# Fetching each expert's tokens by indirect DMA instead of one-hot products in a mixture-of-experts kernel, with the weight splits on fixed engines

## The chip, the cores and the metric

The kernel runs on one core of a Trainium2 chip, in one launch. Its time is the device time of a whole execution in microseconds (us). The core has TensorE (PE, matrix products, with a separate row PEld for its weight loads), VectorE (DVE), ScalarE (ACT), GpSimd (POOL) and SyncE (SP, which here only issues DMAs). DMAs issued by SP go through queue q1 of the profile, those issued by GpSimd through queue q0.

## The reference, cut to what matters

The whole model is two transformer-like blocks over 512 latent tokens and 256 context tokens of width 1024. The change lies in the mixture of experts at the end of the first block. Each token chooses one of 4 groups and 2 of the 4 experts in it; every expert is a gated MLP of width 512:

```
gates = sum(one_hot(expert_id, 16) * top_w)          # (512, 16), two entries a token
for e in range(16):
    a = silu(t @ w_gate[e]) * (t @ w_up[e])          # 1024 -> 512
    y = y + gates[:, e:e + 1] * (a @ w_down[e])      # 512 -> 1024
```

## The kernel before, in words

**Precision.** Every fp32 product is made of three fp32r products. An operand x is split into a high part (a rounded copy of x) and a low part (x minus the high part), and `mm3` (L526 to L530) multiplies high by high, high by low and low by high. So each weight that comes from DRAM is split on the chip before it is used: `unit` (L507) takes a loaded 1 MB unit of weights and cuts it into two pieces of 128x1024; for each piece `split` (L265) makes the high part `whi` (L268 on ScalarE, or L270 on another engine) and then the low part `wlo` (L271). `split_on` is a list of engine pairs that the pieces use in turn. In the expert stage it has four entries, so that of four pieces one has its high part made by VectorE and one has its low part made by GpSimd; ScalarE makes the other high parts and VectorE the other low parts.

**Buffers.** Loaded units lie in 6 buffers of 1 MB (`wraw`, `wrawx`), the split pieces in 4 buffers each of `whi` and `wlo`. SP issues the load of a unit when its buffer comes free; that is the order written in the program, so a load that waits holds those behind it. Three units of gate and up weights for the first experts are loaded ahead (`self.early`).

**The router stage** (`moe`, L1343 to L1372) makes the normalised tokens h (feature by feature), turns them token by token on TensorE and keeps them in SBUF as a high part `hthi` (`hhi`, 4 blocks of 128 tokens by 1024 features) and a low part `htlo`. It then computes the router's choices: `posm` is for each token and expert its place among that expert's tokens (or -1), and `tw` holds token numbers and weights. An expert takes up to 128 tokens at a time, in 128 slots; more than 128 tokens go through `moe_overflow`, a loop whose count is read on the chip (none in the profiled data; the engines meet at the branch).

**The expert stage** (L1442 to L1470) takes the 16 experts in pairs. For a pair, `gather(e)` builds one-hot matrices of tokens by slots (`slot_onehot`, L1237, VectorE). `gather_slots` (L1241) then multiplies `hthi` and `htlo` by them on TensorE: 8 feature blocks, 2 parts and 4 token blocks, so 64 products of 256 columns (128 slots of two experts), whose results ScalarE (six of eight) and VectorE (two of eight) copy to `sxg`. `slot_rows` (L1307) makes from the same one-hots, with 4 products and 2 small transposes, each slot's token number `sri` and weight `srw`. For each expert `hidden` (L1258) makes 48 products of 512 columns for gate and up (8 pieces of weights), `turned` (L1279) transposes the result, and `down` (L1290) makes 24 products (4 pieces), scales the two halves by the slot's weight on ScalarE and VectorE (L1302, L1303), and adds the 128 rows of 4 KB to `ysd` in DRAM by an indirect DMA from GpSimd's queue (L1304). The loop runs `hidden` of expert e+1 between `turned` and `down` of expert e. `late` (after expert 13) reloads the context's normalised tokens, 2 MB, into the memory of `hthi`.

**Order.** The order of the instructions on each engine's queue is fixed when the program is built, by a scheduler that models their times; engines work through their queues in that order.

Of the kernel before, what the change touches and what calls it, by code (L numbers as in the profile page):

```python
# [21 lines left out]
P = 128  # L22
# [201 lines left out]
class Kern:  # L224
# [1016 lines left out]
    def gather_slots(self, pool, oh, hh, name):  # L1241

        nc = self.nc
        n = oh.shape[2]
        x = []
        for k in range(KD):
            if k % 2 == 0:
                x.append(pool.tile([P, 2, 2, n, P], F32R, name=name + "xg", bufs=4))
            p = self.ps.tile([P, 2, n * P], F32, name="aux", tag="aux")
            for i in range(2):  # L1250
                for j in range(4):
# [6 lines left out]
    def hidden(self, pool, x, i, wg, wu, bufs=2):  # L1258

        nc = self.nc  # L1260
        pp = []
        for w in (wg, wu):
            p = self.mmp.tile([P, 512], F32, name="mm")
            for k0 in (0, 4):
                for kp, m, whi, wlo in self.unit(w, k0, 4, [(0, 512)]):
                    for k in range(m):
                        kk = k0 + kp + k
                        xk = x[kk // 2][:, kk % 2]
                        self.mm3(p, xk[:, 0, i, :], xk[:, 1, i, :], whi[:, k, :], wlo[:, k, :], kk == 0, kk == 7)
# [20 lines left out]
    def down(self, pool, a, wd, ysd, slot, bufs=2):  # L1290
# [12 lines left out]
        nc.vector.tensor_scalar(y[:, 512:], py[1], slot[1], None, op0=ALU.mult)  # L1303
# [3 lines left out]
    def slot_rows(self, pool, oh, tw, name):  # L1307
# [14 lines left out]
        for i in range(n):  # L1322
            v = p[:, i, 3 * i:3 * i + 3]
            w = pool.tile([P, 2], F32, name=name + "rw", bufs=4)
            nc.vector.tensor_scalar(w[:, 1:2], v[:, 0:1], 0.0, self.c["part"], op0=ALU.is_equal, op1=ALU.mult)
            row = pool.tile([P, 1], I32, name=name + "ri", bufs=4)
# [5 lines left out]
    def moe(self, dp, hhi, late, ysd, x, bs, mod, fill):  # L1332
# [8 lines left out]
        hh = [hhi, rp.tile([P, 4, D], F32R, name="htlo")]  # L1341
        with self.phase():
# [4 lines left out]
            for i, b in enumerate(bs):  # L1347
                j0, ts = 2 * i, slice(i * 256, i * 256 + 256)
                for k in range(KD):
# [10 lines left out]
                    if k % 2:  # L1360
                        at = lambda t: t[:, j0:j0 + 2, (k - 1) * P:(k + 1) * P]
                        self.split(at(hh[0]), at(hh[1]), p.rearrange("p j k e -> p j (k e)"))
# [78 lines left out]
        self.moe_overflow(dp, hh, ysd, tw, posm, ovl)  # L1441
        with self.phase():  # L1442
            ep = self.pool("exp", 1)
            self.split_on = [(None, None), (None, None), (None, nc.gpsimd), (nc.vector, None)]

            def gather(e):
                oh = self.slot_onehot(ep, posm[:, :, e:e + 2], "s")
                yield self.gather_slots(ep, oh, hh, "s")
                yield self.slot_rows(ep, oh, tw[:, :, e:e + 2, :], "s")
            w = self.weights  # L1450
            xg, rows = gather(0)
            *_, a = self.hidden(ep, xg, 0, w("w_gate", 0), w("w_up", 0))
            for e in range(16):
                slot, g, steps = rows[e % 2], None, None
                if e % 2 and e < 15:
                    g = gather(e + 1)
                    xg = next(g)
                if e < 15:
                    steps = self.hidden(ep, xg, (e + 1) % 2, w("w_gate", e + 1), w("w_up", e + 1))
                    if not g:  # L1460
                        next(steps)
                at = self.turned(ep, a)
                if g:
                    rows = next(g)
                if steps:
                    *_, a = steps
                self.down(ep, at, w("w_down", e), ysd, slot)
                if e == 13:
                    late()
            self.split_on = [(None, None)]  # L1470
# [21 lines left out]
    def moe_overflow(self, dp, hh, ysd, tw, posm, ovl):  # L1492
# [5 lines left out]
        with tc.If(nov > 0), self.phase():  # L1498
# [8 lines left out]
            with tc.For_i(0, nov) as i, self.phase():  # L1507
# [10 lines left out]
                x = self.gather_slots(lp, oh, hh, "o")  # L1518
                w = lambda n: self.weights(n, e)
                *_, a = self.hidden(lp, x, 0, w("w_gate"), w("w_up"), 1)  # L1520
# [361 lines left out]
def build(tc, aps):  # L1882
    nc = tc.nc
    with ExitStack() as ctx:
# [14 lines left out]
        ysd = sd.tile([T + P, D], F32, name="ysd")  # L1899
        mn = K.vec("mix_norm_2", 0, 8)  # L1900
        with K.phase():
# [80 lines left out]
            with K.phase(4):  # L1982
# [6 lines left out]
                for j in range(5):  # L1989
                    nc.sync.dma_start(ysd[j * P:j * P + P, :], z)  # L1990
                xc, accc = K.load_x(cp, aps["ctx_2"], TC, "xcT")
# [12 lines left out]
        with K.phase():  # L2004
            K.wlp = K.pool("wl", 4)
            with K.phase(5, 0, 4):
                K.moe(sd, hhi, reload_hc, ysd, x, bs, mod, lambda pool: ada0(K.matvec_steps, range(5, 6), pool, 2, True))
# [72 lines left out]
```

## Time and profile before

| | |
|---|---|
| median of 3 runs | 2445.67 us (2443.76 to 2450.09) |
| the profiled execution | 2448.05 us, of which the span from first to last instruction is 2446.0 us |
| busy over the span | PE 94%, DVE 69%, ACT 47%, POOL 30% |
| mean granted TensorE clock | 0.981 of full speed |
| expert stage | from about 777 us to the last indirect DMA's issue at 1158.5 us |

Busy shares of the whole span are averages over stages with different limits; what matters for the change is the expert stage, a sixth of the span. The pages give, for a stretch, how many us each engine was busy and the mean share of time that the 16 DMA engines were busy. The spans of products overlap, since they are pipelined: the pace of TensorE is read from the distance of their starts.

### The profile page before, as it was taken

What the parts mean: (1) busy time and instruction counts of PE and PEld (TensorE: products, weight loads), DVE (VectorE), ACT (ScalarE), POOL (GpSimd) and SP (SyncE); (2) the same over time, 40 slices, a digit from 0 to 9 for tenths busy, and PEclk for the clock granted to TensorE, in tenths of its full rate; (3) what the DMA queues carried; (4) which work ended last, traced back from release to release, by engine and by line L of the source; (5) the groups of instructions that cost most, each with busy time, mean ns of one, the idle gap of its engine ahead of it and who ended that gap; (6) DMA issues with size and microseconds to landing.
All of it is one profiled execution on the core that took longest, in us unless ns stands there. A gap on an engine that the chain in (4) does not pass through costs nothing.

```text
span 2446.0 us, 36705 instructions
## 1 busy us (share of the span) xinstructions
PE 2294.4 (94%) x14498; PEld 1975.1 (81%) x14498; DVE 1694.9 (69%) x2552; ACT 1159.8 (47%) x1910; POOL 737.0 (30%) x502
## 2 busy tenths in 40 slices
PE   6998989989987999998999999999999999999998
PEld 4988978768875777777997888877888998888887
DVE  4777877778855999998684884897483435653553
ACT  4454654456753555555435764432343333442443
POOL 2124544345331445444160333232333001010111
PEclk9999999999998999999999999999999999999999
DMA  8563003251054788898410003566343222223221
GB/s 310 180 222 136 27 27 124 79 208 42 2 186 168 269 307 292 294 306 296 150 62 13 1 1 121 196 216 218 137 147 112 91 101 72 87 82 116 91 84 58
DMA packets 65390, 344.40 MB, mean 141 GB/s; under 512 B 7728, under 2 KB 12480, under 8 KB 33984
## 3 DMA queue, kind: packets, MB, share of 16 engines
q1 hardware_dynamic: 62032, 331.32, 37.5%
q0 software_dynamic: 3184, 10.72, 2.7%
q8 instruction: 115, 1.88, 0.3%
q14 instruction: 59, 0.48, 0.1%
HBM read 326.06 MB, written 16.78 MB: 140 GB/s over the span
## 4 chain that ended last, share of the span: by engine, by line
PE 49%; DVE 12%; issue 4%; POOL 2%; ACT 1%; DMA 0%; SPq 0%; POOLq 0%; DVEq 0%; ACTq 0%
PE mm L529 14%; PE mm L530 14%; PE mm L528 13%; DVE wlo L271 4%; DVE mva L383 2%; PE aux L1252 2%; DVE whi L270 1%; PE sc L1578 1%; PE av L1721 1%; PE aux L1596 1%; PE av L1712 1%; POOL ysd L1304 1%; POOL wlo L271 1%; DVE smax L1585 1%; DVE cy L1835 0%
## 5 line engine op out<-in xcount | busy, mean ns | idle before, releaser
L528 PE MATMUL mm<-hhi,whi 128*128 128x512 f32 (+1 forms) x1184 | 438.9, 375 | 10.1 <-ACT whi L268 5.3
L529 PE MATMUL mm<-hlo,whi 128*128 128x512 f32 (+1 forms) x1184 | 442.3, 375 | 2.9 <-DVE hlo L480 2.9
L530 PE MATMUL mm<-hhi,wlo 128*128 128x512 f32 (+1 forms) x1184 | 439.8, 374 | 0.0
L271 DVE TENSOR_TENSOR wlo<-wraw,whi 128x1024 fp32r<-128x1024 f32 (+1 forms) x187 | 271.6, 1461 | 176.1 <-ACT whi L268 174.3
L268 ACT CAST whi<-wraw 128x1024 fp32r<-128x1024 f32 (+1 forms) x224 | 231.9, 1038 | 331.3 <-PE mm L529 229.9
L271 DVE TENSOR_TENSOR wlo<-wrawx,whi 128x1024 fp32r<-128x1024 f32 (+1 forms) x158 | 220.7, 1423 | 96.7 <-ACT whi L268 95.3
L268 ACT CAST whi<-wrawx 128x1024 fp32r<-128x1024 f32 (+1 forms) x178 | 185.4, 1043 | 213.3 <-PE mm L530 105.6
L530 PE MATMUL mm<-whi,hlo 128*128 128x256 f32 x960 | 275.0, 289 | 4.8 <-DVE hlo L480 4.6
L529 PE MATMUL mm<-wlo,hhi 128*128 128x256 f32 x960 | 275.2, 288 | 4.1 <-DVE wlo L271 4.1
L528 PE MATMUL mm<-whi,hhi 128*128 128x256 f32 x960 | 274.1, 287 | 5.3 <-ACT hhi L479 2.6
L528 PEld LDWEIGHTS mm<-hhi,whi 128*128 128x128 f32 x1184 | 225.6, 192 | 49.0 <-ACT whi L268 5.9
L529 PEld LDWEIGHTS mm<-hlo,whi 128*128 128x128 f32 x1184 | 226.9, 192 | 41.3 <-DVE hlo L480 3.3
L530 PEld LDWEIGHTS mm<-hhi,wlo 128*128 128x128 f32 x1184 | 226.2, 191 | 37.9 <-issue 0.2
L271 POOL TENSOR_TENSOR wlo<-wraw,whi 128x1024 fp32r<-128x1024 f32 (+1 forms) x53 | 148.4, 2799 | 262.7 <-ACT whi L268 218.9
L528 PEld LDWEIGHTS mm<-whi,hhi 128*128 128x128 f32 x960 | 186.5, 195 | 6.8 <-ACT whi L268 3.1
L530 PEld LDWEIGHTS mm<-whi,hlo 128*128 128x128 f32 x960 | 186.0, 195 | 7.3 <-DVE hlo L480 6.6
L529 PEld LDWEIGHTS mm<-wlo,hhi 128*128 128x128 f32 x960 | 186.7, 195 | 5.1 <-DVE wlo L271 5.0
L271 POOL TENSOR_TENSOR wlo<-wrawx,whi 128x1024 fp32r<-128x1024 f32 (+1 forms) x52 | 138.4, 2662 | 167.6 <-ACT whi L268 167.6
L1845 POOL TENSOR_TENSOR cy<-cy,csg 128x512 f32<-128x512 f32 x44 | 62.5, 1420 | 351.4 <-DVE cy L1837 342.4
L383 DVE SCALAR_TENSOR_TENSOR mva<-mvr,cc_c,mva 128x512 f32<-128x512 f32 x154 | 156.1, 1013 | 2.4 <-DMA mvr<-in_w_mod_dram 0.2
L529 PE MATMUL mm<-alo,whi 128*128 128x512 f32 (+1 forms) x396 | 145.1, 367 | 0.0
L528 PE MATMUL mm<-ahi,whi 128*128 128x512 f32 (+1 forms) x396 | 144.7, 366 | 0.0
(548 smaller groups left out, 4964.4 us busy)
## 6 DMA issues: line engine op xcount, KB each, us to landing
wrawx<-in_w_down_dram SPq DMA_DIRECT2D x32, 1024.0 KB, 5.2
wrawx<-in_w_gate_dram SPq DMA_DIRECT2D x30, 1024.0 KB, 5.0
wraw<-in_w_up_dram SPq DMA_DIRECT2D x30, 1024.0 KB, 5.0
wraw<-in_ffn_w_up_dram SPq DMA_DIRECT2D x30, 1024.0 KB, 4.9
mvr<-in_ada_w_dram SPq DMA_DIRECT2D x56, 512.0 KB, 4.5
wraw<-in_ada_w_dram SPq DMA_DIRECT2D x20, 1024.0 KB, 5.5
wraw<-in_w_in_dram SPq DMA_DIRECT2D x18, 1024.0 KB, 6.8
mvr<-in_w_mod_dram SPq DMA_DIRECT2D x32, 512.0 KB, 4.2
```

The source lines that it names most:

```text
L268: nc.scalar.copy(hi, src)
L270: hi_eng.tensor_copy(hi, src)
L271: (lo_eng or nc.vector).tensor_sub(lo, src, hi.bitcast(F32))
L383: nc.vector.scalar_tensor_tensor(acc, raw[:, k, :], c, acc, op0=ALU.mult, op1=ALU.add)
L528: nc.tensor.matmul(out, ahi, bhi, start=start, stop=False)
L529: nc.tensor.matmul(out, ahi, blo, start=False, stop=False)
L530: nc.tensor.matmul(out, alo, bhi, start=False, stop=stop)
L1252: nc.tensor.matmul(p[:, i, :], hh[i][:, j, k * P:k * P + P], oh[:, j].rearrange("p n s -> p (n s)"), start=j == 0, stop=j == 3)
L1304: nc.gpsimd.indirect_dma_start(out=ysd, out_offset=bass.IndirectOffsetOnAxis(ap=slot[0], axis=0), in_=y, in_offset=None, compute_op=ALU.add)
L1578: nc.tensor.matmul(s[:, a:a + n], qs[:, qt * P:qt * P + P], ks[i][:, a:a + n], start=i == 0, stop=i == 1)
L1585: nc.vector.tensor_reduce(m, s[:, :768], axis=AX.X, op=ALU.max, negate=True)
L1845: nc.gpsimd.tensor_mul(y, y, sg)
```

## The change

Tokens are no longer gathered by products. The router stage keeps no high and low parts of the turned tokens; it copies them once in fp32 (`ht`, on ScalarE) and stores them to a new DRAM tensor `hd` (four DMAs of 512 KB on SP's queue). Per pair of experts the one-hots and `slot_rows` stay, for the row numbers. With these, `gather_slots` issues one indirect DMA per expert on GpSimd's queue, which reads 128 rows of 4 KB from `hd` into `xt` (2 buffers); a slot without a token reads a row of zeros, stored once beforehand. `slots_feature` turns `xt` feature by feature with 8 transposes on TensorE and splits the result from PSUM into high parts (ScalarE) and low parts (VectorE), two operations of 128x512 each. The gathers are issued for the pair after the next expert, so about one expert ahead of their use. `split_on` is no longer set in this stage: all high parts of weights are made by ScalarE, all low parts by VectorE. Both halves of an expert's result are scaled on ScalarE. `late` moves from after expert 13 to after expert 1. The diff, cut to its core:

```diff
-    def gather_slots(self, pool, oh, hh, name):
...
-                    nc.tensor.matmul(p[:, i, :], hh[i][:, j, k * P:k * P + P], oh[:, j].rearrange("p n s -> p (n s)"),
-                                     start=j == 0, stop=j == 3)
-            dst = x[-1][:, k % 2].rearrange("p i n s -> p i (n s)")
-            (nc.vector.tensor_copy if k % 4 == 3 else nc.scalar.copy)(dst, p)
-        return x
+    def gather_slots(self, pool, hd, row, bufs=2):
+
+        xt = pool.tile([P, D], F32, name="xt", bufs=bufs)
+        self.nc.gpsimd.indirect_dma_start(out=xt, out_offset=None, in_=hd,
+                                          in_offset=bass.IndirectOffsetOnAxis(ap=row, axis=0))
+        return xt
+
+    def slots_feature(self, pool, xt, bufs=2):
+
+        nc = self.nc
+        hi, lo = (pool.tile([P, KD, P], F32R, name="xg" + n, bufs=bufs) for n in ("hi", "lo"))
+        for k0 in (0, 4):
+            p = self.ps.tile([P, 4, P], F32, name="aux", tag="aux")
+            for k in range(4):
+                nc.tensor.transpose(p[:, k, :], xt[:, (k0 + k) * P:(k0 + k + 1) * P], self.ident)
+            self.split(hi[:, k0:k0 + 4, :], lo[:, k0:k0 + 4, :], p)
+        return hi, lo
...
-        nc.vector.tensor_scalar(y[:, 512:], py[1], slot[1], None, op0=ALU.mult)
+        nc.scalar.mul(y[:, 512:], py[1], slot[1])
...
-        hh = [hhi, rp.tile([P, 4, D], F32R, name="htlo")]
+        ht = rp.tile([P, 4, D], F32, name="ht")
...
-                        self.split(at(hh[0]), at(hh[1]), p.rearrange("p j k e -> p j (k e)"))
+                        nc.scalar.copy(ht[:, j0:j0 + 2, (k - 1) * P:(k + 1) * P], p.rearrange("p j k e -> p j (k e)"))
+                for j in (j0, j0 + 1):
+                    nc.sync.dma_start(hd[j * P:j * P + P, :], ht[:, j, :])
...
-            self.split_on = [(None, None), (None, None), (None, nc.gpsimd), (nc.vector, None)]
+            rows, xts = [], []
 
             def gather(e):
...
+                oh = self.slot_onehot(ep, posm[:, :, e:e + 2], "s", 1)
+                two = self.slot_rows(ep, oh, tw[:, :, e:e + 2, :], "s")
+                rows.extend(two)
+                xts.extend(self.gather_slots(ep, hd, row) for row, _ in two)
             w = self.weights
-            xg, rows = gather(0)
-            *_, a = self.hidden(ep, xg, 0, w("w_gate", 0), w("w_up", 0))
+            gather(0)
+            xg = self.slots_feature(ep, xts[0])
+            steps = self.hidden(ep, xg, w("w_gate", 0), w("w_up", 0))
+            next(steps)
+            xg = self.slots_feature(ep, xts[1])
+            gather(2)
+            *_, a = steps
             for e in range(16):
...
                 if e < 15:
+                    steps = self.hidden(ep, xg, w("w_gate", e + 1), w("w_up", e + 1))
+                    next(steps)
                 at = self.turned(ep, a)
+                if e < 15:
+                    next(steps)
+                if e < 14:
+                    xg = self.slots_feature(ep, xts[e + 2])
+                if e % 2 and e < 12:
+                    gather(e + 3)
+                if e < 15:
                     *_, a = steps
+                self.down(ep, at, w("w_down", e), ysd, rows[e])
+                if e == 1:
                     late()
```

The loop of `moe_overflow` uses the same two functions; its body does not run on this data.

## Rows read from the trace of the kernel before

**Rows 1.** Windows: busy us and instructions of each engine, clock, DMA share, GB/s.

```profile
930.00:976.00 46.00, 43.59 (x224) 35.42 (x223) 44.47 (x41) 25.13 (x31) 22.45 (x9) 1.00 0.87 297
```

**Rows 2.** Groups of VectorE, 838 to 1022 us: busy us, mean ns, idle before.

```profile
L271 DVE TENSOR_TENSOR wlo<-wrawx,whi 128x1024 fp32r<-128x1024 f32 x48 | 72.8, 1556 | 0.4
L271 DVE TENSOR_TENSOR wlo<-wraw,whi 128x1024 fp32r<-128x1024 f32 x24 | 49.8, 2098 | 1.4 <-ACT whi L268 1.1
L270 DVE CAST whi<-wrawx 128x1024 fp32r<-128x1024 f32 x16 | 24.0, 1498 | 1.9 <-PE mm L530 1.9
L1303 DVE TENSOR_SCALAR ey<-mm,srw 128x512 f32<-128x512 f32 x8 | 6.0, 747 | 1.9 <-PE mm L530 1.9
L1255 DVE CAST sxg<-aux 128x512 fp32r<-128x512 f32 x8 | 5.5, 688 | 0.7 <-PE aux L1252 0.7
L270 DVE CAST whi<-wraw 128x1024 fp32r<-128x1024 f32 x8 | 5.5, 688 | 0.0
...
L271 DVE TENSOR_TENSOR ealo<-aux,eahi 128x512 fp32r<-128x512 f32 x8 | 5.4, 677 | 0.0
```

**Rows 3.** Groups of ScalarE, 838 to 1022 us.

```profile
L268 ACT CAST whi<-wrawx 128x1024 fp32r<-128x1024 f32 x49 | 51.5, 1051 | 40.5 <-PE mm L530 40.5
L268 ACT CAST whi<-wraw 128x1024 fp32r<-128x1024 f32 x24 | 25.2, 1049 | 26.9 <-PE mm L530 23.3 <-DVE soh L1237 3.6
L1255 ACT CAST sxg<-aux 128x512 fp32r<-128x512 f32 x24 | 13.5, 581 | 1.3 <-PE aux L1252 1.3
L1302 ACT ACTIVATE ey<-mm,srw 128x512 f32<-128x512 f32 x8 | 5.5, 688 | 9.3 <-PE mm L530 9.3
```

**Rows 4.** Waits of SP's queue, 760 to 1170 us: total us, times, longest.

```profile
SPq L504 <- POOL wlo L271: 170.2, 46, 7.0
SPq L504 <- DVE wlo L271: 170.1, 88, 10.3
```

**Rows 5.** Timeline of TensorE in the expert stage.

```profile
784.27 0.40 PE L528 MATMUL mm<-whi,sxg 128*128 128x512 f32 x1
...
905.12 0.39 PE L530 MATMUL mm<-whi,sxg 128*128 128x512 f32 x1
...
906.48 0.39 PE L530 MATMUL mm<-whi,sxg 128*128 128x512 f32 x1
...
919.87 0.60 PE L1284 MATMUL aux<-cst,ea 128*128 128x128 f32 x4
```

**Rows 6.** Timeline of VectorE and GpSimd: start us, us, operation, idle before.

```profile
851.67 2.46 DVE L271 TENSOR_TENSOR wlo<-wraw,whi 128x1024 fp32r<-128x1024 f32 x2
851.78 2.55 POOL L1304 DMA_INDIRECT ysd<-ey,sri  x1 [6.09 <-DVE whi L270]
...
920.57 4.23 DVE L271 TENSOR_TENSOR wlo<-wraw,whi 128x1024 fp32r<-128x1024 f32 x1
...
920.74 2.97 POOL L271 TENSOR_TENSOR wlo<-wrawx,whi 128x1024 fp32r<-128x1024 f32 x1
```

**Rows 7.** The line of the indirect DMA: duration ns min/median/max, first and last start.

```profile
L1304 POOL DMA_INDIRECT ysd<-ey,sri x16: 1552/1770/2562, 825.7 to 1158.5; - x16
...
DMA to landing us min/median/max: 6.0/6.9/11.1
```

**Rows 8.** DMA queues, 838 to 1022 us: packets, MB, share of 16 engines.

```profile
q1 hardware_dynamic: 6885, 50.11, 71.8%
q0 software_dynamic: 1152, 4.19, 14.3%
```

**Rows 9.** DMA queues, 10 to 40 us.

```profile
DMA packets 2569, 12.43 MB, mean 414 GB/s; under 512 B 293, under 2 KB 293, under 8 KB 1505
...
q1 hardware_dynamic: 2560, 12.42, 101.1%
```

**Rows 10.** Timelines of VectorE and SP around the stage's begin.

```profile
777.14 1.29 DVE L1237 TENSOR_TENSOR soh<-cst,posm 128x512 fp32r<-128x512 f32 x2 [3.54 <-PEq L1498]
...
782.54 3.72 SPq L504 DMA_DIRECT2D wraw<-in_w_up_dram  x2
```

More of the change, by code (lines that the diff above doesn't have):

```diff
@@ L1239, in slot_onehot, with hidden @@
         return oh
-    def gather_slots(self, pool, oh, hh, name):
-        nc = self.nc
[L1244 to L1251, printed above, removed]
-                    nc.tensor.matmul(p[:, i, :], hh[i][:, j, k * P:k * P + P], oh[:, j].rearrange("p n s -> p (n s)"),
-                                     start=j == 0, stop=j == 3)
-            dst = x[-1][:, k % 2].rearrange("p i n s -> p i (n s)")
-            (nc.vector.tensor_copy if k % 4 == 3 else nc.scalar.copy)(dst, p)
-        return x
-    def hidden(self, pool, x, i, wg, wu, bufs=2):
+    def gather_slots(self, pool, hd, row, bufs=2):
[4 more added lines that the diff above has]
+    def slots_feature(self, pool, xt, bufs=2):
+        nc = self.nc
+        hi, lo = (pool.tile([P, KD, P], F32R, name="xg" + n, bufs=bufs) for n in ("hi", "lo"))
[5 more added lines that the diff above has]
+        return hi, lo
+    def hidden(self, pool, x, wg, wu, bufs=2):
         nc = self.nc
@@ L1323, in slot_rows @@
             v = p[:, i, 3 * i:3 * i + 3]
-            w = pool.tile([P, 2], F32, name=name + "rw", bufs=4)
+            w = pool.tile([P, 2], F32, name=name + "rw", bufs=6)
             nc.vector.tensor_scalar(w[:, 1:2], v[:, 0:1], 0.0, self.c["part"], op0=ALU.is_equal, op1=ALU.mult)
-            row = pool.tile([P, 1], I32, name=name + "ri", bufs=4)
+            row = pool.tile([P, 1], I32, name=name + "ri", bufs=6)
             nc.vector.scalar_tensor_tensor(row, v[:, 0:1], float(T), w[:, 1:2], op0=ALU.add, op1=ALU.add)
@@ L1330, in slot_rows, with moe @@
         return out
-    def moe(self, dp, hhi, late, ysd, x, bs, mod, fill):
+    def moe(self, dp, late, ysd, hd, x, bs, mod, fill):
         nc, tc = self.nc, self.tc
@@ L1450, in moe @@
             w = self.weights
-            xg, rows = gather(0)
-            *_, a = self.hidden(ep, xg, 0, w("w_gate", 0), w("w_up", 0))
+            gather(0)
[5 more added lines that the diff above has]
+            *_, a = steps
             for e in range(16):
[L1454 to L1457, printed above, removed]
@@ L1458, in moe @@
                 if e < 15:
-                    steps = self.hidden(ep, xg, (e + 1) % 2, w("w_gate", e + 1), w("w_up", e + 1))
-                    if not g:
-                        next(steps)
+                    steps = self.hidden(ep, xg, w("w_gate", e + 1), w("w_up", e + 1))
+                    next(steps)
                 at = self.turned(ep, a)
-                if g:
-                    rows = next(g)
-                if steps:
+                if e < 15:
+                    next(steps)
@@ L1490, in moe_add, with moe_overflow @@
                 nc.tensor.matmul(sums[:, j, :], sq[:, j * P:j * P + P], w2[:, k, :], start=k + j == 0, stop=k + j == 10)
-    def moe_overflow(self, dp, hh, ysd, tw, posm, ovl):
+    def moe_overflow(self, dp, hd, ysd, tw, posm, ovl):
         nc, tc = self.nc, self.tc
@@ L1517, in moe_overflow @@
                 rows = self.slot_rows(lp, oh, pm[:, 4:].rearrange("p (j e c) -> p j e c", e=1, c=3), "o")
-                x = self.gather_slots(lp, oh, hh, "o")
+                x = self.slots_feature(lp, self.gather_slots(lp, hd, rows[0][0], 1), 1)
                 w = lambda n: self.weights(n, e)
-                *_, a = self.hidden(lp, x, 0, w("w_gate"), w("w_up"), 1)
+                *_, a = self.hidden(lp, x, w("w_gate"), w("w_up"), 1)
                 self.down(lp, self.turned(lp, a, 1), w("w_down"), ysd, rows[0], 1)
@@ L1899, in build @@
         ysd = sd.tile([T + P, D], F32, name="ysd")
+        hd = sd.tile([T + P, D], F32, name="hd")
         mn = K.vec("mix_norm_2", 0, 8)
@@ L1990, in build @@
                     nc.sync.dma_start(ysd[j * P:j * P + P, :], z)
+                nc.sync.dma_start(hd[T:, :], z)
                 xc, accc = K.load_x(cp, aps["ctx_2"], TC, "xcT")
@@ L2006, in build @@
             with K.phase(5, 0, 4):
-                K.moe(sd, hhi, reload_hc, ysd, x, bs, mod, lambda pool: ada0(K.matvec_steps, range(5, 6), pool, 2, True))
+                K.moe(sd, reload_hc, ysd, hd, x, bs, mod, lambda pool: ada0(K.matvec_steps, range(5, 6), pool, 2, True))
             qp, st = right(qstack, "qst"), right(astack, "astore")
```

12 lines of the change are left out of this document (2 added, 10 removed).

## The prediction

> **What bounds the kernel now.** I read the stretches of the expert stage first, then the groups of each engine in four pairs of experts, then the timeline of one pair, and last the DMA queues. In the stretches the reader is to see that three resources are close to full at once: in 46 us VectorE is busy 44.5, TensorE 43.6 and the DMA engines 0.87 of the time, while ScalarE with 25.1 and GpSimd with 22.5 have room [rows 1]. In 184 us VectorE makes 72 low parts and 24 high parts of weights and ScalarE 73 high parts [rows 2, 3], so 96 pieces are four pairs of experts of 24 pieces: a pair takes 46.0 us.
>
> The next question is which of the three is the cause. SP's loads wait for buffers, half for GpSimd's low parts and half for VectorE's [rows 4]; so DMA is not it, it is made to wait. TensorE's own work is shorter than it looks, because spans overlap: six products of 512 columns start within 906.48 - 905.12 = 1.36 us, 0.227 us each [rows 5]; the 144 products of a pair are 32.7 us, the 64 gather products of half as many columns about 7.3 (an estimate: half of 0.227 each), 8 transposes at 0.60 / 4 = 0.15 us are 1.2, and slot_rows' four products about 0.5: 41.7 of 46. VectorE is the one with no slack, and much of its time is not work. A low part of 128x1024 takes 1.23 us when GpSimd only issues an indirect DMA beside it (two in 2.46 us), and 4.23 us beside one of GpSimd's subtractions of 2.97 us [rows 6]. The mean is 1.56 us from one kind of buffer and 2.10 from the other; VectorE's high parts take 0.69 or 1.50 us [rows 2]. So GpSimd's help with every fourth low part is paid for by VectorE.
>
> **The change part by part, for one pair.**
>
> VectorE. The 18 low parts cost (72.8 + 49.8) / 4 = 30.7 us now; 24 at 1.23 are 29.5. Six high parts go: (24.0 + 5.5) / 4 = 7.4. The result's scaling goes: 1.5. Two copies of gathered tokens go: 1.4. Four low parts of gathered tokens from PSUM come, at 0.68 as the hidden's low part: 2.7 [rows 2]. Sum: 44.5 - 1.2 - 7.4 - 1.5 - 1.4 + 2.7 = 35.7 us. One-hots and slot_rows stay.
>
> TensorE. 64 gather products go (7.3), 16 transposes at 0.15 come (2.4): 41.7 - 7.3 + 2.4 = 36.8 us [rows 5].
>
> ScalarE. Six high parts at 1.05 come (6.3), two scalings at 0.69 (1.4), four high parts of tokens at 0.58 (2.3), six copies go (3.5): 25.1 + 6.5 = 31.6 us [rows 1, 3]. It has waited for TensorE to free buffers, and keeps 9 us of slack.
>
> GpSimd. Six subtractions go, two gathers come. It issues four indirect DMAs a pair, at 1.55 to 2.56 us each [rows 7]: at most 10 us, with nothing else in its queue. What is queued behind a gather there is the scatter of an expert's result, for which nobody waits until the stage's end.
>
> DMA. This is the part that decides. Queue q1 moves 50.11 MB in four pairs, 12.53 MB a pair; at 71.8% of 184 us that is 33.0 us of all 16 engines. The scatters take 14.3%, 26.3 us for eight: 3.3 us each, although each is only 0.52 MB [rows 8]. A gather of 0.52 MB appears nowhere in this trace. From below: where loads queue without a gap (10 to 40 us), with 4 KB packets among them, 12.42 MB take 1.011 of 30 us, 0.41 MB per us, so a gather takes 1.3 us [rows 9]. From above: it costs what a scatter of the same bytes costs, 3.3 us. The scatter reads, adds and writes to DRAM; the gather only reads DRAM and writes SBUF like any load, so the load is its nearest row, and I take 1.4. For the weights the bounds are 33.0 us, as now, and 12.53 / 0.41 = 30.6 with full queues; I take the middle, 31.8, because SP will no longer wait most of the time. Sum: 31.8 + 6.6 + 2.8 = 41.2 us; bounds 30.6 + 6.6 + 2.6 = 39.8 and 33.0 + 6.6 + 6.6 = 46.2.
>
> So with VectorE at 35.7, TensorE at 36.8 and ScalarE at 31.6, the DMA engines are next, and a pair takes 41.2 us: 4.8 less. Over eight pairs that is -38.4 us.
>
> One rule of the Trainium skill speaks against the gathers. First the row: an indirect DMA on GpSimd takes 2.55 us beside two of VectorE's subtractions [rows 6] and 1.55 at best [rows 7], so VectorE costs it 1.0 us. The Trainium skill's page "SBUF — State Buffer", section "SBUF: two separate sides", says that descriptors of DMAs from GpSimd's queue cannot be written while VectorE holds the port pair that both use, so that such a DMA looks blocked. By the row the four issues are 10 us in a free queue and cost nothing; by the rule each waits for VectorE's running operation to end, which matters only if a gather then comes late, and that is the late-gather rival below.
>
> The stage's begin. Now the one-hots start at 777.14 and the first product of the hidden layer at 784.27, 7.1 us later [rows 5, 10]. After the change the chain is one-hots (1.3 us), slot_rows (about 2.5 us, an estimate: four short products, one copy, two transposes and three small operations with their hand-overs), the gather (6.0 to 11.1 us from issue to landing for scatters; I take 6.9 [rows 7]), eight transposes of which the first four are needed (0.6), high and low part (1.3): 12.6 us, +5.5. It could be 4.6 to 9.8.
>
> `late`. Its 2.1 MB are the same bytes, but where DMA is the bound they are no longer free: 2.1 / 0.41 = +5.1 us, wherever in the stage they stand.
>
> The router stage. Eight subtractions of VectorE at about 0.68 go; ScalarE and TensorE set the pace there with the chain of tokens, so I count -1, between 0 and -5. Four stores of 0.5 MB join SP's queue; after its loads ahead SP issues nothing until 782.54 [rows 10], so they are covered; without that cover they would take 2.1 / 0.41 = 5 us before the first gather.
>
> Sum: -38.4 + 5.5 + 5.1 - 1 = -28.8 us. The profiled execution took 2448.05 us, so 2419; it lies 2.4 above the median of the runs, 2445.67, against which the forecast stands: 2417 us.
>
> **The rivals.**
>
> Compute pace. If full queues move weights at 0.41 MB per us, DMA needs 39.8 us a pair, hardly more than TensorE's 36.8 with its waits, and `late` fits beside. For it: 30 us at that rate [rows 9]. Against: that stretch has no scatters between the loads. Time: 8 x 6.2 = -49.6, + 5.5 - 1 = -45, so 2401 us.
>
> Gathers as dear as scatters (slower). If the short rows or the second queue, not the adding, make the scatter slow, a gather takes 3.3 us and a pair 46.2 us. Then the stage gains nothing (+1.6) and pays 5.5 + 5.1 - 1: +11, 2457 us. The point of no gain is a pair of 44.8 us, which is a gather of 2.6 us with the weights at 33.0. For it: the only indirect DMA of the trace moves bytes at less than half of the loads' rate [rows 8]. Against: it is the only one that adds.
>
> Late gather. TensorE works in order; if the transposes of an expert's tokens come to the front before the gather has landed, everything behind them stands. The first gather of a pair is issued about one expert (20.6 us) ahead: slot_rows with its waits about 5 us, issue 2.6, landing up to 11.1 [rows 7] is 18.7, so it just fits. It takes away the gain if it lands 3.6 us late or more in each pair beyond that slack (28.8 / 8); 8 us late would give 8 x 8 - 29 = +35, 2481 us.
>
> Not what it says. VectorE's low parts could stay slow, if GpSimd's DMA issue held them too. The pair of subtractions beside an issue took 2.46 us [rows 6], so this is nearly excluded.
>
> **How the numbers follow.** The measurement tells 0.3%, 7.3 us, from no change; so faster is below 2438, slower above 2453. DMA pace 41.2 us, 2407 to 2430: 0.45. Compute pace, 2392 to 2407: 0.25. Between 2430 and 2438 (gathers of some 2 us): 0.08. Gathers of about 2.6 us and more up to no change: 0.12. Dear gathers, slower: 0.07. Late gather: 0.03. So faster 0.78, same 0.12, slower 0.10. The range, 2393 to 2443, leaves out some 0.05 below and some 0.14 above. The likeliest case alone has 2407 to 2430.
>
> **What would show it.** In the profile of the changed kernel: low parts of weights on VectorE at 1.2 us throughout; VectorE busy about 36 us in a pair's time and no longer 97% of it; DMA share at 0.95 or more over the middle of the stage, and SP's loads waiting less; the last scatter issued near 1130 instead of 1158.5; gathers at 1.3 to 2 us of DMA time each; the first product of the hidden layer near 790. If the DMA share stays at 0.87 with a shorter pair, the compute pace was right; if it is full at 46 us a pair, the gathers are dear; if TensorE's transposes of `xt` wait for a DMA, the gather is late. A changed order outside the stage would make the sum wrong without touching its steps.

## The result, and the profile after

The changed kernel takes 2402.05 us (2399.18 to 2404.64), the kernel before beside it 2447.37 us (2443.76 to 2450.09): a ratio of 0.9821, 95% interval 0.9808 to 0.9834, or 45.3 us less. The forecast was 2417 us, faster, between 2393 and 2443. The direction and the range hold; the value lies 15 us below the likeliest case and at the rival called "Compute pace" (2401 us). Whether for that rival's reasons, the rows and runs below must say.

Stretches of the expert stage in the changed kernel come first, one from a scatter's issue to that of the second expert after it, then some of 40 us. Columns: the stretch and its length, busy us (and instructions) of PE, PEld, DVE, ACT and POOL, the granted clock, the DMA share, GB/s.

```profile
844.52:881.92 37.40, 37.07 (x176) 29.97 (x175) 33.71 (x40) 29.50 (x36) 10.68 (x4) 1.00 1.02 386
```

```profile
800.00:840.00 40.00, 40.00 (x190) 32.20 (x189) 38.32 (x51) 33.16 (x39) 9.49 (x5) 1.00 0.94 350
840.00:880.00 40.00, 39.67 (x189) 32.12 (x188) 37.03 (x44) 31.68 (x38) 12.84 (x5) 1.00 1.01 388
880.00:920.00 40.00, 38.55 (x178) 30.05 (x176) 34.71 (x43) 31.16 (x39) 17.91 (x5) 1.00 0.98 368
920.00:960.00 40.00, 30.76 (x134) 24.65 (x135) 26.98 (x34) 24.00 (x30) 6.75 (x3) 0.87 0.86 297
1040.00:1080.00 40.00, 39.31 (x182) 31.65 (x181) 36.55 (x36) 33.12 (x40) 3.20 (x2) 1.00 1.02 393
```

The first line is a pair of experts where nothing goes wrong: it takes 37.4 us, and in it TensorE is busy 37.07 and the DMA share is 1.02. The row that answers to it before had 46 us, VectorE at 44.5 and a share of 0.87 [rows 1]. In the second fence the reader is to see the line that falls out: from 920 to 960 us every engine does less, TensorE has 134 products in place of some 180, the clock is 0.87, and the DMA share too falls to 0.86.

The groups of VectorE and ScalarE, 840 to 1000 us (busy us, mean ns of one, idle before and its releaser):

```profile
L271 DVE TENSOR_TENSOR wlo<-wrawx,whi 128x1024 fp32r<-128x1024 f32 x61 | 72.1, 1216 | 8.7 <-ACT whi L268 8.3
L271 DVE TENSOR_TENSOR wlo<-wraw,whi 128x1024 fp32r<-128x1024 f32 x31 | 36.3, 1213 | 4.9 <-ACT whi L268 4.9
L271 DVE TENSOR_TENSOR xglo<-aux,xghi 128x512 fp32r<-128x512 f32 x16 | 10.5, 683 | 10.8 <-ACT xghi L268 10.8
```

```profile
L268 ACT CAST whi<-wrawx 128x1024 fp32r<-128x1024 f32 x59 | 60.5, 1054 | 9.9 <-PE mm L530 9.4 <-DVE wlo L271 0.3
L268 ACT CAST whi<-wraw 128x1024 fp32r<-128x1024 f32 x32 | 32.5, 1054 | 5.9 <-PE mm L530 5.9
```

A low part takes 1.21 to 1.22 us throughout, where it took 1.56 and 2.10 [rows 2]. VectorE now waits for ScalarE's high parts, and ScalarE for TensorE only 15 us in 160, against 64 in 184 [rows 3].

The DMA queues in the same 160 us, then the lines of the scatter and of the gather (duration ns min/median/max, first and last start):

```profile
q1 hardware_dynamic: 6522, 47.48, 75.9%
q0 software_dynamic: 2294, 8.37, 20.1%
```

```profile
L1304 POOL DMA_INDIRECT ysd<-ey,sri x16: 1555/1612/13194, 826.5 to 1112.7; - x16
```

```profile
L1244 POOL DMA_INDIRECT xt<-hd,sri x16: 970/1480/7238, 785.2 to 1036.2; - x16
```

The last scatter is issued at 1112.7 us, 45.9 us earlier than before [rows 7]; so the whole gain arises ahead of it. But one scatter's issue took 13.2 us, against at most 2.56 before.

**Where the 45 us came from.** I divide the stage at the first product of the hidden layer: the begin runs from the first one-hots to it, and the pace is the time from it to the last scatter's issue, divided by eight pairs. Before: 777.14, 784.27 and 1158.53 us [rows 5, 7, 10], a begin of 7.1 us and 46.8 us a pair. After: 776.41, 792.88 and 1112.65, a begin of 16.5 and 40.0 a pair. Eight pairs give -54.5, the begin +9.3: -45.2 us.

Timelines of the changed kernel follow: VectorE at the begin, GpSimd at the begin and around 901 us, TensorE's two waits for gathered tokens.

```profile
776.41 1.29 DVE L1237 TENSOR_TENSOR soh<-cst,posm 128x512 fp32r<-128x512 f32 x2 [2.04 <-DVEq L1504]
777.78 2.36 DVE L271 TENSOR_TENSOR wlo<-wraw,whi 128x1024 fp32r<-128x1024 f32 x2
780.06 0.41 DVE L1317 COPY srs<-aux 6x256 f32<-6x256 f32 x1
780.39 1.27 DVE L1237 TENSOR_TENSOR soh<-cst,posm 128x512 fp32r<-128x512 f32 x2
781.60 2.34 DVE L271 TENSOR_TENSOR wlo<-wraw,whi 128x1024 fp32r<-128x1024 f32 x2
783.87 0.20 DVE L1325 TENSOR_SCALAR srw<-aux,cst 128x1 f32<-128x1 f32 x1
```

```profile
785.19 1.08 POOL L1244 DMA_INDIRECT xt<-hd,sri  x1 [34.84 <-DMA wraw<-in_w_up_dram]
...
901.37 13.19 POOL L1304 DMA_INDIRECT ysd<-ey,sri  x1 [17.83 <-DVE srs L1317]
914.87 1.10 POOL L1244 DMA_INDIRECT xt<-hd,sri  x1 [0.30 <-issue]
916.27 0.97 POOL L1244 DMA_INDIRECT xt<-hd,sri  x1 [0.31 <-issue]
```

```profile
790.41 2.82 PE L1255 MATMUL aux<-cst,xt 128*128 128x128 f32 x12 [9.51 <-DMA xt<-hd,sri]
792.88 0.66 PE L528 MATMUL mm<-whi,xghi 128*128 128x512 f32 x1
```

```profile
928.46 1.97 PE L1255 MATMUL aux<-cst,xt 128*128 128x128 f32 x8 [8.97 <-DMA xt<-hd,sri]
```

Two things are to be seen. At the begin the small operations of `slot_rows` stand in VectorE's queue behind two pairs of weight subtractions and the next pair's one-hots, so the first gather is issued 8.8 us after the first one-hots, and TensorE waits 9.5 us. And at 901.37 the scatter's issue holds GpSimd for 13.2 us; both gathers of a pair are queued behind it, and at 928.46 TensorE has waited 9.0 us for them. Behind that wait its clock stands at the lower level, 1.2 GHz, a granted share of 0.50, and is back at 1.00 only from 936:

```profile
928.46:932.00 3.54, 3.54 (x13) 3.15 (x14) 1.38 (x2) 2.12 (x4) 0.00 (x0) 0.50 0.88 181
932.00:936.00 4.00, 4.00 (x16) 3.19 (x15) 3.98 (x4) 2.94 (x3) 0.00 (x0) 0.85 0.12 19
936.00:940.00 4.00, 4.00 (x19) 3.03 (x17) 1.96 (x3) 2.86 (x4) 0.00 (x0) 1.00 0.94 387
```

### The profile page after: what moved, and what is told of

Same layout as the page of the kernel before. It is cut to its first block, busy times and chain, and to the rows that moved or that the text cites. A ratio compares the mean times of both kernels' runs of the same rounds, so it can differ in the third digit from the quotient of the medians.

```text
span 2402.4 us, 35932 instructions
## 1 busy us (share of the span) xinstructions
PE 2248.2 (94%) x14114; PEld 1932.2 (80%) x14114; DVE 1620.0 (67%) x2544; ACT 1199.1 (50%) x1958; POOL 644.3 (27%) x470
## 4 chain that ended last, share of the span: by engine, by line
PE 44%; DVE 5%; issue 1%; ACT 1%; POOL 0%; DMA 0%; SPq 0%; POOLq 0%; DVEq 0%; ACTq 0%
PE mm L530 13%; PE mm L529 13%; PE mm L528 13%; PE sc L1584 1%; PE av L1727 1%; PE aux L1602 1%; DVE mva L383 1%; PE av L1718 1%; DVE smax L1591 1%; DVE wlo L271 0%; ACT pexp L1593 0%; DVE cy L1841 0%; DVE nmt L477 0%; PE aux L1573 0%; DVE z L1806 0%
## 5 line engine op out<-in xcount | busy, mean ns | idle before, releaser
L268 ACT CAST whi<-wraw 128x1024 fp32r<-128x1024 f32 (+1 forms) x240 | 246.2, 1041 | 276.2 <-PE mm L529 223.4
L271 DVE TENSOR_TENSOR wlo<-wraw,whi 128x1024 fp32r<-128x1024 f32 (+1 forms) x203 | 255.2, 1273 | 187.2 <-ACT whi L268 185.8
L271 DVE TENSOR_TENSOR wlo<-wrawx,whi 128x1024 fp32r<-128x1024 f32 x190 | 229.1, 1230 | 101.8 <-ACT whi L268 100.5
L268 ACT CAST whi<-wrawx 128x1024 fp32r<-128x1024 f32 (+1 forms) x210 | 215.8, 1046 | 154.1 <-PE mm L529 105.2
L529 PEld LDWEIGHTS mm<-hlo,whi 128*128 128x128 f32 x1184 | 226.7, 192 | 41.2 <-DVE hlo L480 3.3
L530 PE MATMUL mm<-ahi,wlo 128*128 128x512 f32 (+1 forms) x396 | 144.4, 365 | 0.0
L271 POOL TENSOR_TENSOR wlo<-wraw,whi 128x1024 fp32r<-128x1024 f32 (+1 forms) x37 | 90.8, 2454 | 198.9 <-ACT whi L268 184.5
```

Source lines behind the costliest of these rows:

```text
L268: nc.scalar.copy(hi, src)
L271: (lo_eng or nc.vector).tensor_sub(lo, src, hi.bitcast(F32))
L529: nc.tensor.matmul(out, ahi, blo, start=False, stop=False)
L530: nc.tensor.matmul(out, alo, bhi, start=False, stop=stop)
```

## The experiments

The profiled executions differ by up to 10 us in what follows the stage: from the last scatter's issue to the end of the span it is 1287.5 us before, 1289.8 after, and 1285.9 to 1296.0 in the experiments. They differ ahead of it too: in the two profiles of the changed kernel the first one-hots start at 776.4 and at 769.9 us. So beside each time stand begin, pace and the stage's length (first one-hots to the last scatter's issue) from the profile. All ratios are against the kernel before on the same chip.

| kernel | us (median) | ratio, 95% | begin | pace | stage |
|---|---|---|---|---|---|
| before | 2447.4 | | 7.1 | 46.8 | 381.4 |
| changed | 2402.1 | 0.9821 [0.9808, 0.9834] | 16.5 | 40.0 | 336.2 |
| changed, again | 2402.6 | 0.9826 [0.9813, 0.9840] | 17.3 | 40.2 | 338.7 |
| e1 old splits | 2450.6 | 1.0017 [1.0007, 1.0028] | 17.4 | 45.0 | 377.2 |
| e2 splits only | 2413.8 | 0.9869 [0.9853, 0.9886] | 8.1 | 42.1 | 345.1 |
| e9 GpSimd's low parts | 2428.6 | 0.9929 [0.9905, 0.9953] | 17.8 | 42.8 | 360.4 |
| e3 gathers ahead | 2397.7 | 0.9798 [0.9779, 0.9818] | 17.6 | 38.5 | 325.5 |
| e8 first pair early too | 2386.9 | 0.9759 [0.9742, 0.9775] | 11.9 | 38.7 | 321.7 |
| e4 = e8 without scatters | 2383.4 | 0.9751 [0.9732, 0.9770] | 11.9 | 37.8 | 314.2 |
| e5 = e8, two products | 2376.8 | 0.9720 [0.9700, 0.9739] | 11.9 | 36.9 | 307.4 |
| e6 = e8, gathers twice | 2394.8 | 0.9796 [0.9777, 0.9815] | 16.3 | 40.1 | 336.8 |
| e10 changed, memsets | 2406.6 | 0.9842 [0.9829, 0.9856] | 17.2 | 39.7 | 335.1 |
| e11 = e8, memsets | 2391.8 | 0.9783 [0.9767, 0.9800] | 11.9 | 39.7 | 329.2 |

**Which half of the change made the gain.** My theory after the result: VectorE was the bound, so the splits come first, and the gathers add only what they take from TensorE once VectorE is relieved. The rival: the gathers made the gain. e1 is the changed kernel with the old list, e2 the kernel before with the new one:

```diff
# e1, in the expert stage of the changed kernel
+            self.split_on = [(None, None), (None, None), (None, nc.gpsimd), (nc.vector, None)]
# e2, in the kernel before
-        nc.vector.tensor_scalar(y[:, 512:], py[1], slot[1], None, op0=ALU.mult)
+        nc.scalar.mul(y[:, 512:], py[1], slot[1])
-            self.split_on = [(None, None), (None, None), (None, nc.gpsimd), (nc.vector, None)]
+            self.split_on = [(None, None)]
```

> The changed kernel (2402 us) with the old list of split engines back in the expert stage: one low part in four on GpSimd, one high part in four on VectorE; gathers stay indirect DMAs and both halves of the expert output are scaled on ScalarE. Theory A (the splits are the larger part of the gain, because VectorE was the bound with subtractions of 1.5 to 2.1 us beside GpSimd's): VectorE comes to about 43 us a pair again, against the 39.9 us that the changed kernel takes, so 8 x 3 = 25 us come back, 2425 to 2440 us. Theory B (the indirect gathers alone made the gain, by taking 5 us of TensorE's work from each pair): 2402 to 2412 us.

> The kernel before (2447 us) with the new list of split engines alone, and the second half of the expert output scaled on ScalarE; the gather by one-hot products stays. Theory A: VectorE falls from 44.5 to about 36 us a pair and TensorE, with 41.7 us of work a pair, is next; with its small waits 43 us a pair against 46, so 2447 - 24 = 2423 us (2418 to 2430). Theory B (gathers alone made the gain): 2440 to 2450 us.

The gathers alone gain nothing: 2450.6 us, 4 us slower than before and 10 us above what my theory expected. The splits alone give 2413.8, 32 us faster and 4 us below the range that it expected. One stretch of e1, then one of e2:

```profile
840.00:880.00 40.00, 34.50 (x155) 25.83 (x154) 39.14 (x36) 22.68 (x27) 21.94 (x10) 1.00 0.94 327
```

```profile
840.00:880.00 40.00, 40.00 (x214) 33.91 (x213) 31.99 (x36) 29.65 (x36) 3.12 (x2) 1.00 0.95 322
```

In e1 VectorE is busy 39.14 of 40 us and TensorE 34.5: the 5 us a pair that the gathers take from TensorE are taken from an engine that waits, the pace falls only from 46.8 to 45.0, 14 us in eight pairs. The longer begin takes 10 of them back, and what is left of the shorter stage is lost behind it (1295.7 us from the last scatter to the end, 1287.5 before). VectorE is not that full all through e1: in the stretches of 40 us from 880 to 1080 it is busy 32.6 to 37.9. But what TensorE waits for is VectorE's pieces: 35.5 us in all from 780 to 1160, against 9.0 for GpSimd's, and it waits for gathered tokens only at the begin. In e2 TensorE is busy 40.00 of 40: it is the bound, at 42.1 us a pair, and there the gathers' relief counts. The two parts don't add: -32 and +4 alone, -45 together.

**The two halves of VectorE's relief.** e9 leaves every high part on ScalarE but gives GpSimd its quarter of the low parts back, so it tells the moved high parts from GpSimd's interference.

```diff
# in the expert stage of the changed kernel
+            self.split_on = [(None, None), (None, None), (None, nc.gpsimd), (None, None)]
```

> The changed kernel (2402 us) with one low part in four back on GpSimd and every high part left on ScalarE. It tells the two halves of the VectorE relief apart: high parts moved off VectorE, and GpSimd's subtractions taken away from beside it. Theory S (the shared slow-down is the larger half): VectorE has 18 low parts a pair at 1.7 us, as in the kernel before, and with the 7 us of the rest 37.7 us; but the gathers and scatters also queue behind GpSimd's subtractions and late gathers stall TensorE, so 2408 to 2425 us. Theory M (moving the high parts is what counts): VectorE at 18 parts has enough room and the time stays within 4 us of 2402.

2428.6 us: 26.6 above the changed kernel, 22 below e1, so, taken in this order, GpSimd's low parts account for 27 us and the moved high parts for 22. M falls. S has VectorE's part right, but not the late gathers that it added: behind the begin TensorE waits for none in e9, and the time lies 4 us above its range. VectorE's groups of low parts in e9, 840 to 1000 us, and TensorE's waits, 800 to 1090 us:

```profile
L271 DVE TENSOR_TENSOR wlo<-wrawx,whi 128x1024 fp32r<-128x1024 f32 x47 | 75.0, 1628 | 8.9 <-ACT whi L268 8.8
L271 DVE TENSOR_TENSOR wlo<-wraw,whi 128x1024 fp32r<-128x1024 f32 x22 | 34.1, 1572 | 9.0 <-ACT whi L268 7.1 <-issue 1.6
```

```profile
PE mm L529 <- DVE wlo L271: 11.8, 14, 2.4
PE mm L529 <- POOL wlo L271: 10.6, 9, 3.1
```

Beside GpSimd's subtractions (2.7 us each) VectorE's 18 low parts a pair take 1.6 us, so 29 us, as long as all 24 take it alone. So GpSimd's help is worth nothing to VectorE, and TensorE now also waits for GpSimd's own pieces.

**What the late gathers cost.** e3 gives the gathered tokens a third buffer (one of the hidden activation pays for it) and issues each gather two experts ahead; e8 also moves the first pair's one-hots, slot rows and gathers in front of the branch on overflowing experts, out of the weight subtractions' way.

```diff
# e3
-        xt = pool.tile([P, D], F32, name="xt", bufs=bufs)
+        xt = pool.tile([P, D], F32, name="xt", bufs=3 if bufs == 2 else 1)
...
-                if e % 2 and e < 12:
-                    gather(e + 3)
+                if e < 11:
+                    gather(e + 5)
# e8, further
+            gather(0)
+            gather(1)
             self.moe_overflow(dp, hd, ysd, tw, posm, ovl)
+            ep = self.pool("exp", 1)
+            gather(2)
```

> The changed kernel with three buffers for gathered tokens in place of two (one buffer for the hidden activation pays for it), and each gather issued about two experts ahead of its use in place of one. Theory: the wait of 9.0 us of TensorE before 928.46 us, with the low clock behind it about 12 us, is paid because both gathers of a pair stood behind a scatter whose issue was held for 13.2 us; with the gathers already landed it goes, and the time falls by 8 to 13 us, to 2389 to 2394 us. Rival (the DMA engines bound the stage, at a share of 0.98 to 1.02 around the wait): the weights have then to come in less time, SP's loads are as late, and the time stays within 3 us of 2402.

> The kernel with gathers two experts ahead, and the one-hots, slot rows and gathers of the first two experts put before the branch on overflowing experts (with the buffers that this takes) in place of behind it. Theory: the chain from the first one-hots to the first hidden product, 16.5 us in the changed kernel with 9.5 us of it TensorE waiting for the first gathered tokens, starts 2 to 3 us earlier and no longer has weight subtractions of 2.4 us each in between: 6 to 9 us less than with gathers ahead alone, about 2383 us. Rival (the begin is bound by the first weights or by the branch): no more than 2 us less than with gathers ahead alone.

In e3's stage the theory holds: TensorE waits for a gather only at the begin, the pace is 38.5, and the stage is 10.7 us shorter. Of that only 4.4 us reach the time, which lies above the expected 2389 to 2394: the profiled execution took 1296.0 us from the last scatter to its end, 6 more than the changed kernel. One of e3's four executions took 2390.6, the others 2397.5 to 2398.9; what takes those 6 us after the stage I did not find. e8 takes 2386.9 us, 15 less than the changed kernel and 10.8 less than e3, where 6 to 9 were expected (and 2383 us). Its begin is 5.7 us shorter and its stage 3.8; the rest of the 10.8 lies outside the stage. It is the fastest of the versions that leave nothing out.

**Which resource sets the pace now.** Theory D (DMA, my prediction's likeliest case) against P (TensorE), on e8, which has no late gathers:

```diff
# e4: no scatter for experts 0 to 14 (slot[2] is set for them)
+        if bufs == 2 and slot[2]:
+            return
         nc.gpsimd.indirect_dma_start(out=ysd, out_offset=bass.IndirectOffsetOnAxis(ap=slot[0], axis=0), in_=y,
...
# e5: `hidden` and `down` call mm2 in place of mm3; low of the activation x high is left out
+    def mm2(self, out, ahi, alo, bhi, blo, start, stop):
+        nc = self.nc
+        nc.tensor.matmul(out, ahi, bhi, start=start, stop=False)
+        nc.tensor.matmul(out, ahi, blo, start=False, stop=stop)
# e6
+        for _ in range(bufs):
             self.nc.gpsimd.indirect_dma_start(out=xt, out_offset=None, in_=hd,
```

> The kernel with gathers two experts ahead and the first pair before the branch (2387 us), with the scatters of experts 0 to 14 left out (their outputs are computed and dropped). Theory D (the DMA engines bound the stage, at a share of 1.01 and 38.7 us a pair in the steady part): a scatter is about 2.6 us of all 16 DMA engines, so 5.2 us a pair go and TensorE, busy 38.8 of 40 us, is next at about 37 us a pair: 8 to 16 us less, 2371 to 2379 us. Theory P (TensorE bounds the stage and the DMA engines just keep up): within 4 us of 2387.

> The same kernel of 2387 us, with one of the three products of each expert matmul left out (low part of the activation by high part of the weight), so a third of TensorE's expert work. Theory D (the DMA engines bound): TensorE's 37 us a pair fall to about 26, the pair keeps its 38 to 39 us, and only the last expert's tail without gathers and the begin are shorter: 2377 to 2389 us. Theory P (TensorE bounds): the pair falls to VectorE's 35 us, about 3.5 x 8 = 28 us less, 2355 to 2365 us.

> The same kernel of 2387 us, with every gather of the stage issued twice into the same buffer, one behind the other. Price of a gather taken in the prediction: 1.4 us of all 16 DMA engines, 2.8 us a pair. Theory D (the DMA engines bound): 16 x 1.4 = 22 us more, less what the begin hides: 2400 to 2410 us. Theory P (TensorE bounds and the DMA engines have room): 2387 to 2392 us. If a gather cost as much as a scatter took before (3.3 us): 2430 us or more.

Neither theory comes out whole. Without 15 scatters the time is only 3.5 us shorter, inside P's 4 us and below D's 8 to 16, but the stage is 7.5 us shorter and the pace 37.8, which P does not explain. With a third of TensorE's products gone the time is 2376.8, where D had 2377 to 2389; the pace is 36.9, not the 35 of P, and the DMA share is 1.02, in these two stretches of e5 as in the one between:

```profile
920.00:960.00 40.00, 33.36 (x135) 23.68 (x134) 35.32 (x43) 31.02 (x39) 13.96 (x4) 0.87 1.02 397
...
1000.00:1040.00 40.00, 31.70 (x127) 22.05 (x127) 35.37 (x35) 33.36 (x41) 4.67 (x3) 0.95 1.02 398
```

One stretch of e4, then one of e6:

```profile
840.00:880.00 40.00, 40.00 (x192) 33.01 (x191) 37.98 (x47) 34.36 (x42) 3.60 (x3) 1.00 0.98 377
```

```profile
920.00:960.00 40.00, 38.83 (x179) 30.18 (x179) 33.88 (x42) 29.97 (x38) 10.41 (x7) 1.00 1.02 396
```

So the DMA engines, with TensorE relieved, seem to need 36.9 us a pair: the bytes say the same, 12.53 MB of weights [rows 8] and four transfers of 0.52 MB are 14.63 MB, at 397 GB/s 36.9 us. The loads say it too: from 840 to 1000 us they land 11.9 to 13.1 us after their issue at the median in e5, 9.4 to 9.8 in e8. And e6 says it from the other side: six transfers make 15.7 MB a pair, at its 396 GB/s 39.6 us, and its pace is 40.1. That the DMA engines alone set the pace of e5 is still argued and not shown: VectorE is busy 35 of 40 us there, TensorE's clock is low at times, and no run takes these away. TensorE, with the DMA engines relieved, needs 37.8 (e4). Together they take 38.7, which fits two resources of nearly equal load that now and then wait for each other.

The time of e6 lies between the two forecasts. Its sixteen gathers more cost 15.1 us of stage (7.9 of the time); 4.4 of it are at the begin, where the first tile waits for both of its gathers, and the rest is 0.8 us for each of the other 14. That is less than my 1.4 us, as it should be where DMA is the bound only part of the time, and far from the 3.3 of a scatter.

**Why GpSimd's issue took 13 us.** On VectorE, from 901 to 914 us, nine weight subtractions with two SBUF operands follow each other, with a one-hot of 0.67 us and six operations of 0.14 to 0.20 us between them; the issue ends shortly after the hidden layer's product with its PSUM operand, at 913.27:

```profile
911.90 1.21 DVE L271 TENSOR_TENSOR wlo<-wrawx,whi 128x1024 fp32r<-128x1024 f32 x1
913.27 0.69 DVE L1276 TENSOR_TENSOR ea<-esg,mm 128x512 f32<-128x512 f32 x1 [0.16 <-PE mm L530]
```

To see whether VectorE's run holds the issue, e10 puts a short operation ahead of every low part, and e11 does it where no gather is late:

```diff
+            if self.gap:
+                self.nc.vector.memset(lo.bitcast(F32)[:, 0:1], 0.0)
             self.split(hi[:, :m * n], lo[:, :m * n], src, he, le)
```

> The changed kernel (2402 us) with a memset of one column on VectorE ahead of every low part of the expert stage (384 of them; the column is overwritten by the low part). Theory H (GpSimd's issue of an indirect DMA is held while VectorE runs subtractions of two SBUF operands back to back, and goes on at the next VectorE operation of another kind): with such an operation at least every 1.3 us no issue takes above 3 us, the scatter at 901 us does not take 13.2 us, the gathers behind it are not late, TensorE does not wait 9 us for them, and the stage ends 8 to 13 us earlier less 1 to 3 us for the memsets' own time: 2391 to 2398 us. Rival (the issue waits for room in the DMA queue, or for the DMA engines): the 13 us stay, and the time is 2402 to 2406 us.

> The changed kernel once more, beside the two with the memsets, for their difference on one chip: 2402 us within 4 us by every theory, and the scatter of the fifth expert near 901 us held for 10 us or more again if that is no chance event.

> The kernel with gathers two experts ahead and the first pair before the branch (2387 us), with the same memsets. Theory H: its issues of up to 3.8 us become 1 to 2 us, but no gather is late there any more, so nothing is left to win and the memsets cost at most 2 us: 2385 to 2390 us. Rival (the holds still cost in that kernel): 2378 to 2384 us.

GpSimd's timeline shows the fifth scatter in the repeated changed kernel, and then, in e10, the same scatter with the two gathers behind it:

```profile
896.54 13.19 POOL L1304 DMA_INDIRECT ysd<-ey,sri  x1 [17.84 <-DVE srs L1317]
```

```profile
907.24 3.67 POOL L1306 DMA_INDIRECT ysd<-ey,sri  x1 [17.78 <-DVE wlo L522]
911.22 1.00 POOL L1246 DMA_INDIRECT xt<-hd,sri  x1 [0.30 <-DVE wlo L522]
912.53 1.93 POOL L1246 DMA_INDIRECT xt<-hd,sri  x1 [0.31 <-PE mm L531]
```

TensorE's waits for gathered tokens in e10, 780 to 1120 us (total, times, longest):

```profile
PE aux L1257 <- DMA xt<-hd,sri: 12.1, 2, 10.2
```

The hold is no chance event: it is 13.19 us both times. With the memsets the longest scatter issue is 3.67 us and the longest gather issue 5.0, and of TensorE's 12.1 us of waiting 10.2 are the begin's; the 9.0 us in the middle have become 1.9. Of the 32 issues two take above 3 us, where seven did. The same gather in e8 and, with the memsets, in e11:

```profile
868.30 3.83 POOL L1244 DMA_INDIRECT xt<-hd,sri  x1 [7.39 <-PE mm L530]
```

```profile
868.18 1.44 POOL L1246 DMA_INDIRECT xt<-hd,sri  x1 [7.43 <-PE mm L532]
```

So the memsets shorten the issues, as H has it, and the rival, under which the 13 us stay, falls. The rest of H does not hold: the 13.19 us outlasted six short operations of other kinds, the issue at 907.24 outlasts two memsets, and a gather's issue of the changed kernel (839.65 us, 3.56 long) ended in the middle of four subtractions. Nor are memsets needed: e3, with the same subtractions in another order, has only one issue above 3 us, of 3.83. What in VectorE's run holds an issue, and what frees it, stays open.

H fails on the time as well: 2406.6, 4 us slower. e11, at 2391.8 above both of its forecasts, gives a reason: there, with no gather late, the memsets cost 7.5 us of stage (from 880 to 1040 us VectorE's memsets wait 11 us at the head of its queue for buffers that TensorE frees). If they cost as much in e10, whose stage is 1 to 4 us shorter than the two changed ones, it saved 9 to 11 us of late gathers and paid 7.5; the time does not show the rest. The cure is the earlier gather, not the gap.

## Why the prediction came out as it did

**What bounded before, and VectorE's term: right.** Low parts at 1.22 us (1.23 taken), in the clean pair VectorE 33.7 us (35.7 taken), ScalarE 29.5 (31.6), GpSimd 10.7 (at most 10). TensorE's 37.1 there is busy time, in which spans overlap; that it needs 37.8 us a pair (36.8 taken) is e4's pace. e1 and e2 show that VectorE was the bound and that TensorE's 42 was next.

**The DMA term: the step that failed.** It was "31.8 + 6.6 + 2.8 = 41.2 us" as a floor under the pair. In the changed kernel the shares still give about that: 75.9% of 160 us for 47.48 MB are 32.0 us for a pair's weights, and 20.1% for 16 transfers 2.0 us each, 8.0 a pair, together 40.1. But a share is the time in which packets are under way, and it is not a price. It stands at 0.95 for 322 GB/s in e2, where TensorE sets the pace, and at 1.02 for 397 GB/s in e5, where the DMA engines seem to. I took the scatter's 3.3 us and half of the weights' 33.0 from queues that were waiting for buffers. At the rate of full queues the floor is 36.9, 4.3 us a pair lower, 34 us in the stage, and so not above TensorE's 37.8: that the DMA engines are next, by 4 us over TensorE, did not come true either. The row for it stood there: 414 GB/s [rows 9] for all 14.63 MB gives 35.3. The rival "Compute pace" took that rate for the weights and the gathers and kept 6.6 for the scatters; so its 39.8 was too high as well, and its 2401 us is right by luck: the late gathers, which it did not have, and the longer begin made up for it.

**The late gather: seen, but priced as a rival only.** I counted 18.7 us from `slot_rows` to the landing, within the 20.6 us of an expert, and gave lateness 3 in 100. The term that was off is the issue, 2.6 us there and 13.2 at 901 us. The Trainium skill's page "SBUF — State Buffer", section "SBUF: two separate sides", gives the SBUF port pair that VectorE and GpSimd share to whichever instruction starts first, for the whole of it; of VectorE operations with two SBUF inputs it says so only against a GpSimd operation that reads SBUF, and that descriptors cannot be written it says of VectorE's 2-port modes. So my reading, that each issue waits for VectorE's running operation to end, went beyond the page, and the trace gives another length: the issue did not get in at the end of one subtraction, it outlasted nine. Of the seven pairs of gathers behind the first, one was so late that TensorE stood still; with the low clock behind it that cost 8 x (40.0 - 38.5) = 12 us of stage by e3, which also has the other issues shorter. The kernel is not slower, as that rival had it, since the other six were in time.

**The begin: +5.5 taken, +9.3 measured**, inside the bounds of 4.6 to 9.8. What I left out is VectorE's queue: `slot_rows` waited behind 4.7 us of weight subtractions.

**`late`: +5.1 taken, none in the stage.** I held that it costs that "wherever in the stage" it stands. SP issued it before the stage, which is possible since nothing in the stage reads `hthi` any more:

```profile
740.29 2.25 SPq L258 DMA_DIRECT2D hthi<-hcdhi  x4
742.99 1.87 SPq L258 DMA_DIRECT2D hthi<-hcdlo  x4
```

**The router stage: -1 taken**; the first one-hots start 0.7 us earlier, but in the repeated changed kernel 7.2, so a term of 1 us cannot be told from the spread.

So the sum was -28.8: -38.4 + 5.5 + 5.1 - 1. The runs say 8 x (38.5 - 46.8) = -66 for the pace, +9.3 for the begin, +12 for the late gathers, nothing for `late` and -0.7 ahead: -45. The gain was forecast some 16 us too small, and the time 15 too high, because a gain of pace that was 28 us too small (41.2 us a pair taken and 38.5 found, 46.0 taken before and 46.8 found) and a term for `late` of 5 were half made up by a stall that I had all but excluded and a begin 4 us longer.

## What to carry to other kernels

Two changes that relieve two resources are worth what the order of the bounds allows: measure each alone, for here the one that saves the matrix work gained nothing until the other had freed VectorE. Price a transfer as bytes over the rate of a stretch in which the queues are full, not as the busy share of a stretch in which loads wait for buffers. A DMA that GpSimd issues can need slack for an issue of 13 us, not 1.5, beside a VectorE that runs SBUF subtractions without a pause; one more buffer and an earlier issue gave it that here, and the stage became 11 us shorter.

## What the runs showed of the hardware that was not expected

An indirect DMA's issue on GpSimd, 1.6 us at the median, took 13.19 us twice at the same scatter, beside VectorE's back-to-back subtractions of two SBUF operands, and at most 5.0 us with short memsets between these; which property of VectorE's run decides is not settled. GpSimd's quarter of those subtractions, 2.7 us each, slowed VectorE's from 1.22 to 1.6 us, so that it took no time off VectorE. And a TensorE with less work can run at a lower clock: in e5, busy 33.4 of 40 us from 920 to 960 us, its mean granted clock was 0.87, so part of the time at the lower level of 1.2 GHz, where e8 with all three products had 1.00 (0.96 at the lowest of its seven stretches from 800 to 1080 us). From 908 to 912 us it stood at 0.50 in e5, behind waits of TensorE of 2.1 us for a high part and 0.5 us for a low part. A stretch of e8, then that of e5:

```profile
920.00:960.00 40.00, 38.71 (x177) 30.15 (x178) 35.48 (x42) 30.44 (x38) 7.60 (x4) 1.00 0.97 355
```

```profile
908.00:912.00 4.00, 4.00 (x10) 3.13 (x11) 4.00 (x4) 3.27 (x4) 0.00 (x0) 0.50 1.03 403
```

What this took back of e5's gain was not measured.
